# A two-layer diffusion backbone: the output projection and the routing in a fixed order on TensorE, and one product of the first context pair moved to GpSimd

## The chip, the cores and the metric

The kernel runs on one core of a Trainium2 chip. The metric is the device time of one execution in microseconds; the same program is run several times and its median is taken. Engines are called as in the profile: PE (TensorE, matrix products and transpositions), DVE (VectorE), ACT (ScalarE), POOL (GpSimd) and SP (SyncE, which only issues DMAs here). Each executes its own instructions strictly in the order in which they stand, and waits for the others by semaphores.

## The reference

One step of a backbone with 2 layers on 512 latent tokens and 128 context tokens, model width 1024. Every layer mixes tokens and then sends them through 16 experts of which each chooses its own tokens (capacity 64 of 512 latents, 16 of 128 context tokens):

```python
mix = jnp.concatenate([a_out, b_out, c_out], axis=-1) @ w_out
x = layer_norm(ALPHA * x + gate1 * mix, ln1_g, ln1_b)
u = x * (1 + scale2) + shift2
x = layer_norm(ALPHA * x + gate2 * expert_choice_ffn(u, ...), ln2_g, ln2_b)

def expert_choice_ffn(u, w_router, w_gate, w_up, w_down):
    cap = CAPACITY_FACTOR * T // N_EXPERTS
    aff = jax.nn.softmax((u @ w_router).astype(jnp.float32), axis=-1)
    g, idx = lax.top_k(aff.swapaxes(1, 2), cap)
    xs = jax.vmap(lambda ub, ib: ub[ib])(u, idx)
    hdn = jax.nn.silu(xs @ w_gate[e]) * (xs @ w_up[e])     # for each expert e
    ye = hdn @ w_down[e] * g
    # ye is added into the rows idx of a zero tensor of T rows
```

The change touches the stage from the product with `w_out` up to the first expert's products, once in each layer.

## The kernel before, in words

The 640 tokens are five tiles of 128: 0 to 3 are latents, 4 (`CTX`) is the context.

**Projection.** `project(t, half)` makes 512 of the 1024 columns of one tile: 8 steps of k with three 128x512 matmuls each (`mm3`, L229 to L232: high by high, high by low, low by high part), 24 in all, into `ps_o`, of which PSUM holds three. `w_out` is split into high and low parts just ahead of it (L226 on ACT, L227 on DVE or POOL): `wo00`, `wo01` are the two halves of k for the left columns, `wo10`, `wo11` for the right ones. Then DVE multiplies with the gate (L859), adds to the row block `xa` (L861, in layer 1 L864) and takes statistics (L867). After the second half the mean and the inverse deviation `bsd` are made (L300, L284 on DVE, L285 on POOL, L322 on DVE).

**Routing of a tile.** `turn(t, g)` transposes four 128x128 blocks of one half of `xa` on PE (L881), ACT copies them out as `u` (L883), and four 32-row matmuls bring the router's sums into `ps_rt` (L887). `route(t)` copies these (`parts`, ACT, L896), adds them over four groups of partitions by a matmul with `fold` (L898), makes a softmax `rex` on DVE and ACT (L900 to L906; L900 needs `bsd`), transposes it (L907) and copies it to the table of affinities (L909). ACT normalises `xa` in place (L323) and the rows are stored to DRAM as `zrow` (L911), from where the chosen rows are gathered. `residual(t)` later scales `xa` in place (L337, L338 on POOL) and writes it to the accumulator (L842); it overwrites `xa` and so has to wait for the store of `zrow`.

**End of the stage.** When tile 3 is routed, DVE finds the best 64 of the 512 latents for each expert (eight rounds of L976, L979, L980); two small transpositions `ps_tc` on PE turn places (`ldup`) and values (`lvd`) into columns, DVE makes the integer list `lgi` (L1041), and POOL gathers rows (`xsl`, L961). While this goes on, PE does gate and up of the first two experts on their context rows: `fill(n)` issues n of eight groups of four 32-row matmuls into `ps_gc`. `ctx_hidden` makes the hidden rows `hc` from `ps_gc` (silu `sc` on ACT, L1161; product on DVE, L1163), `ctx_turn` transposes them (`ps_hcT`, copied to `hcT` by ACT, L1172), and `ctx_rows` does the down product (`ps_dc`, 16 lines of the program, 32 rows in the trace) and scales it (`yc`, DVE, L1184). Then `xsl` is transposed to `xT` (L253, L261 on ACT, L264 on DVE) and the latent products `ps_g`, `ps_u`, `ps_d` of the pair follow. Seven more pairs of experts follow in each layer.

**What sets the order.** The order on each engine is found by a scheduler that simulates the program; an instruction stands where that simulation lets it start. `inline` (L234 to L239) overrides this for PE: each matmul or transposition given to `mm` or `turn1` is issued after the one given before it. In the kernel before, that holds from the start of the experts' stage on only (`line.clear()` at L1070). The projection and the routing are ordered by the scheduler. The order of DVE, ACT, POOL and SP is the scheduler's throughout, apart from a few `issue_after`.

Of the kernel before, what the change touches and what calls it, by code (L numbers as in the profile page):

```python
# [65 lines left out]
def kernel(ctx: ExitStack, tc: tile.TileContext, a: dict):  # L66
# [162 lines left out]
    def mm3(out, lh, ll, rh, rl, first, last):  # L229
        nc.tensor.matmul(out, lhsT=lh, rhs=rh, start=first, stop=False)  # L230
        nc.tensor.matmul(out, lhsT=lh, rhs=rl, start=False, stop=False)  # L231
        nc.tensor.matmul(out, lhsT=ll, rhs=rh, start=False, stop=last)  # L232
# [543 lines left out]
    def out_proj(l, mixA, mixC, w2, ms, mixed):  # L776
        ps_dn = Banks(f"dn{l}", 2)
# [66 lines left out]
        def project(t, half):  # L844
# [26 lines left out]
        stt, lnv, banks = {}, {}, {}  # L871

        def turn(t, g, after=None, then=None):

            if g == 0:
                banks[t] = ps_dn.tile("ps_rt")
            r = 1 if t == CTX else 0
            ps = ptr("tr8").rearrange("p (k n) -> p k n", k=4)
            with tc.issue_after(after.ins) if after else ExitStack():
                for kk in range(4):  # L880
                    ins = nc.tensor.transpose(ps[:, kk, :], xs[t][0][:, 512 * g + kk:512 * g + 512:4], ident)  # L881
            u2 = newhalf("u2").rearrange("p (k n) -> p k n", k=4)
# [8 lines left out]
        def route(t, after=None):
            r = 1 if t == CTX else 0
            xa, (mv, sd), bank = xs[t][0], lnv[t], banks.pop(t)
            pl, pa = bank[:, 256:256 + NE], bank[0:NE, 384:512]
            parts = newhalf("parts")[:, 0:P]
            nc.scalar.copy(out=parts, in_=bank[:, 0:P])  # L896
            with tc.issue_after(after.ins) if after else ExitStack():
                nc.tensor.matmul(pl, lhsT=parts, rhs=fold, start=True, stop=True)  # L898
            ex = st([P, NE], "rex")
            nc.vector.scalar_tensor_tensor(out=ex, in0=pl, scalar=sd[:, 0:1], in1=lb[:, r], op0=ALU.mult, op1=ALU.add)  # L900
            mx = st([P, 1], "rmx")
            nc.vector.tensor_reduce(out=mx, in_=ex, axis=AX.X, op=ALU.max, negate=True)
            sm = st([P, 1], "rsm")
            nc.scalar.activation(out=ex, in_=ex, func=AF.Exp, bias=mx, scale=1.0, accum_out=sm)
            nc.vector.reciprocal(out=sm, in_=sm)
            nc.vector.tensor_scalar(out=ex, in0=ex, scalar1=sm[:, 0:1], scalar2=None, op0=ALU.mult)  # L906
            order["weighed"] = nc.tensor.transpose(pa, ex, ident)  # L907
            dst = afc if t == CTX else afl[32 * (t // 2):32 * (t // 2) + NE, t % 2 * P:(t % 2 + 1) * P]
            nc.vector.tensor_copy(out=dst, in_=pa)  # L909
            normalise(xa, mv, sd, False)  # L910
# [630 lines left out]
```

## Time and profile before

| | |
|---|---|
| runs of the kernel before | 1294.45, 1296.16, 1302.5 us, median 1296.16 |
| profiled execution | 1294.52 us, span 1292.7 us |
| PE busy | 1193.2 us, 92% of the span |
| DVE, ACT, POOL busy | 543.7, 368.3, 252.8 us (42%, 28%, 20%) |
| chain that ended last | PE 84%, DVE 7%, ACT 4%, DMA 2% |
| stage that is changed | layer 0 from 273.7 to about 372 us; layer 1 the same stage up to 983.6 us |

PE is the engine that the end waits for: any time that it stands idle is in the sum unless something after it waits anyway. The stage is best read in stretches, by how busy each engine is in them, and then by its instructions in order of time.

### The profile page before, as it was taken

To read this page: it belongs to the slowest core of one execution; us is meant where nothing else is said; L and a number is where in the kernel's file an instruction comes from. 1 tells how busy PE (TensorE), PEld (TensorE's weight loads), DVE (VectorE), ACT (ScalarE), POOL (GpSimd) and SP (SyncE) were. 2 spreads that over 40 slices of the span, in tenths; PEclk is the share of its full clock that TensorE was granted. 3 is DMA by queue.
4 is the path that set the end of the run, shared out by engine and by line. 5 is a ranking of instruction groups with operands and counts; after the bars stand their busy time and mean duration, and the time that the engine had idled before them with its cause. 6 is when DMAs were issued, how large, how long until landed. Compare 5 with 4: busy or idle time off the path is not lost.

```text
span 1292.7 us, 18180 instructions
## 1 busy us (share of the span) xinstructions
PE 1193.2 (92%) x7244; PEld 710.7 (55%) x7244; DVE 543.7 (42%) x1266; ACT 368.3 (28%) x800; POOL 252.8 (20%) x234
## 2 busy tenths in 40 slices
PE   5999999999879999999969999999987999999994
PEld 1877886987523333333349998798752333333331
DVE  1554464777531121111297756477653111111116
ACT  1532134663411110111145423475341101011111
POOL 0210002004330221121175000200433022012114
PEclk8999999999979999999989999999998999999998
DMA  9868666164869999999543315606487999999932
GB/s 360 310 209 301 226 237 226 69 214 150 339 259 402 397 396 406 410 400 332 193 138 98 86 46 197 242 19 225 157 320 287 406 396 396 410 406 386 357 102 82
DMA packets 85078, 342.34 MB, mean 265 GB/s; under 512 B 18713, under 2 KB 32089, under 8 KB 54401
## 3 DMA queue, kind: packets, MB, share of 16 engines
q1 hardware_dynamic: 73568, 305.96, 61.4%
q0 software_dynamic: 9840, 29.45, 8.4%
q10 hardware_dynamic: 1584, 5.77, 1.1%
q8 instruction: 57, 0.93, 0.3%
q14 instruction: 29, 0.23, 0.1%
HBM read 313.73 MB, written 27.51 MB: 264 GB/s over the span
## 4 chain that ended last, share of the span: by engine, by line
PE 84%; DVE 7%; ACT 4%; DMA 2%; issue 1%; SPq 1%; POOL 0%; POOLq 0%; ACTq 0%; DVEq 0%
PE ps_d L239 9%; PE ps_g L239 9%; PE ps_u L239 9%; PE ps_gc L239 8%; PE ps_dc L239 5%; PE ps_ada L185 4%; PE ps_c L230 3%; PE ps_c L232 3%; PE ps_c L231 3%; PE ps_o L231 3%; PE ps_o L230 3%; PE ps_o L232 3%; PE ps_p L733 1%; PE tr L239 1%; PE ps_b L230 1%
## 5 line engine op out<-in xcount | busy, mean ns | idle before, releaser
L239 PE MATMUL ps_g<-wg,xT 128*64 128x512 f32 x512 | 116.1, 595 | 0.1
L239 PE MATMUL ps_d<-wd,hT 128*64 128x512 f32 x512 | 113.6, 595 | 2.5 <-DVE yc L1184 1.6
L239 PE MATMUL ps_u<-wu,xT 128*64 128x512 f32 x512 | 115.4, 592 | 0.0
L239 PE MATMUL ps_gc<-wu,xc 128*32 128x512 f32 x512 | 115.0, 595 | 0.0
L239 PE MATMUL ps_gc<-wg,xc 128*32 128x512 f32 x512 | 115.0, 594 | 0.0
L1161 ACT ACTIVATE sc<-ps_gc 32x512 f32<-32x512 f32 x32 | 18.8, 587 | 328.8 <-PE ps_gc L239 299.7
L1163 DVE TENSOR_TENSOR hc<-ps_gc,sc 32x512 f32<-32x512 f32 x32 | 22.0, 688 | 174.9 <-ACT sc L1161 174.8
L239 PEld LDWEIGHTS ps_d<-wd,hT 128*64 128x64 f32 x512 | 35.5, 137 | 78.7 <-issue 75.7
L1110 POOL DMA_INDIRECT yaccc<-yc,csi x28 | 39.8, 1421 | 192.5 <-DVE yc L1184 155.0
L239 PEld LDWEIGHTS ps_g<-wg,xT 128*64 128x64 f32 x512 | 36.0, 137 | 75.1 <-issue 72.7
L239 PEld LDWEIGHTS ps_u<-wu,xT 128*64 128x64 f32 x512 | 37.2, 137 | 72.6 <-issue 71.8
L239 PE MATMUL ps_dc<-wd,hcT 128*32 128x512 f32 x512 | 71.1, 705 | 0.9 <-ACT hcT L1172 0.9
L239 PEld LDWEIGHTS ps_gc<-wg,xc 128*32 128x32 f32 x512 | 29.2, 110 | 75.0 <-issue 73.7
L185 PE MATMUL ps_ada<-wada,cs 128*32 128x512 f32 x368 | 60.1, 630 | 4.8 <-DMA wada<-in_w_ada_dram 4.8
L1212 DVE SCALAR_TENSOR_TENSOR ye<-ps_d,lg,gl 128x512 f32<-128x512 f32 x32 | 24.0, 751 | 95.7 <-PE ps_d L239 92.9
L1191 DVE TENSOR_TENSOR h<-ps_u,sg 128x512 f32<-128x512 f32 x16 | 11.1, 692 | 104.1 <-PE ps_u L239 104.1
L261 ACT ACTIVATE xT<-tr,modB,modA 128x128 f32<-128x128 f32 x64 | 28.0, 459 | 60.8 <-DVE xT L264 59.1
L239 PEld LDWEIGHTS ps_dc<-wd,hcT 128*32 128x32 f32 x512 | 17.2, 126 | 43.0 <-issue 39.1
L961 POOL DMA_INDIRECT xsl<-zrow,lgi x16 | 15.9, 991 | 102.3 <-PE tr L239 87.9
L285 POOL TENSOR_TENSOR bsd<-bsd,neg_half 128x1 f32<-128x1 f32 x15 | 9.5, 634 | 128.7 <-DVE bsd L284 128.7
L1184 DVE SCALAR_TENSOR_TENSOR yc<-ps_dc,cg,gc 128x512 f32<-128x512 f32 x16 | 12.0, 749 | 52.9 <-PE ps_dc L239 52.9
L227 POOL TENSOR_TENSOR wo00l<-r_wo,wo00h 128x1024 fp32r<-128x1024 f32 x4 | 10.4, 2610 | 119.4 <-ACT wo00h L226 119.4
(618 smaller groups left out, 2839.0 us busy)
## 6 DMA issues: line engine op xcount, KB each, us to landing
wg<-in_w_gate_dram SPq DMA_DIRECT2D x64, 1024.0 KB, 12.4
wu<-in_w_up_dram SPq DMA_DIRECT2D x64, 1024.0 KB, 14.9
wd<-in_w_down_dram SPq DMA_DIRECT2D x64, 1024.0 KB, 17.8
wada<-in_w_ada_dram SPq DMA_DIRECT2D x46, 1024.0 KB, 7.2
r_wo<-in_w_out_dram SPq DMA_DIRECT2D x8, 1024.0 KB, 8.7
zrow<-xa ACTq DMA_DIRECT2D x8, 512.0 KB, 7.7
yacc<-xa POOLq DMA_DIRECT2D x8, 512.0 KB, 9.9
z<-yacc SPq DMA_DIRECT2D x8, 512.0 KB, 6.2
```

Of the source, the lines that this page charges most:

```text
L185: nc.tensor.matmul(ps[32 * j:32 * j + 32, :], lhsT=cs[:, k, :], rhs=w[:, j * 512:(j + 1) * 512], start=(k == 0), stop=(k == KD - 1))
L230: nc.tensor.matmul(out, lhsT=lh, rhs=rh, start=first, stop=False)
L231: nc.tensor.matmul(out, lhsT=lh, rhs=rl, start=False, stop=False)
L232: nc.tensor.matmul(out, lhsT=ll, rhs=rh, start=False, stop=last)
L239: line["pe"] = op(*args, **kw)
L261: nc.scalar.activation(out=out[:, kk, :], in_=ps[:, kk, :], func=AF.Identity, scale=A[:, r, k:k + 1], bias=B[:, r, k:k + 1])
L733: nc.tensor.transpose(pt[:, kk, i * P:(i + 1) * P], prs[i][:, (k0 + kk) * P:(k0 + kk + 1) * P], ident)
L961: ins = nc.gpsimd.indirect_dma_start(out=x, out_offset=None, in_=src, in_offset=bass.IndirectOffsetOnAxis(ap=idx, axis=0))
L1110: nc.gpsimd.indirect_dma_start(out=acc[:, :], out_offset=bass.IndirectOffsetOnAxis(ap=idx[h][0:64, j:j + 1], axis=0), in_=y[hs], in_offset ...
L1161: nc.scalar.activation(out=sc[64 * i + 32:64 * i + 64], in_=pc[64 * i:64 * i + 32], func=AF.Silu)
L1163: nc.vector.tensor_tensor(out=hc[32 * i:32 * i + 32], in0=pc[64 * i + 32:64 * i + 64], in1=sc[64 * i + 32:64 * i + 64], op=ALU.mult)
L1212: order["ye"] = nc.vector.scalar_tensor_tensor(out=ye[:, hs], in0=pd, scalar=lg[:, j:j + 1], in1=gl2[:, hs], op0=ALU.mult, op1=ALU.mult)
```

## The change

- `mm3` takes the function that issues its matmuls, and `project` gives it `mm`: all of the projection's matmuls, transpositions and routing matmuls now stand in one written order on PE, from the start of the stage (`line.clear()` is moved there).
- The routing's steps become functions that `project` calls at given steps of k: `turn(t, 0)` at k=4 and `match(t, 0)` (the router's sums) at k=6 of `project(t, 1)`; `turn(t, 1)` and `match(t, 1)` at k=4 and k=6 of the next tile's first half; `weigh` (fold and softmax) at k=0 and `listed` (affinities, normalising, store) at k=5 of its second half. For tile 3 the second half's steps stand between the groups of `fill`.
- The context rows' modulation is divided between DVE and ACT (it was on ACT alone).
- For the first pair, ACT copies the up rows out of PSUM (`uc`), and POOL multiplies them with `sc` into `hc`. The product no longer waits for `lgi`; the scaling `yc` does instead.

```diff
-    def mm3(out, lh, ll, rh, rl, first, last):
-        nc.tensor.matmul(out, lhsT=lh, rhs=rh, start=first, stop=False)
+    def mm3(out, lh, ll, rh, rl, first, last, put=nc.tensor.matmul):
+        put(out, lhsT=lh, rhs=rh, start=first, stop=False)
...
-                mm3(ps, mh[:, k], ml[:, k], wh[:, k % 4], wl[:, k % 4], k == 0, k == KD - 1)
+                for step in between.get(f"k{k}", ()):
+                    step()
+                mm3(ps, mh[:, k], ml[:, k], wh[:, k % 4], wl[:, k % 4], k == 0, k == KD - 1, mm)
...
         project(CTX, 0)
-        project(CTX, 1)
-        turn(CTX, 0)
-        project(0, 0)
-        router(CTX)
...
+        project(CTX, 1, k4=[turn(CTX, 0)], k6=[match(CTX, 0)])
+        for t in range(4):
+            p = t - 1 if t else CTX
+            spare = t in (2, 3)
+            project(t, 0, k1=[ctx_row(t - 2, 0)] if spare else [], k4=[turn(p, 1)], k6=[match(p, 1)])
+            project(t, 1, k0=[weigh(p)], k1=[ctx_row(t - 2, 1)] if spare else [], k4=[turn(t, 0)],
+                    k5=[listed(p)] + ([] if t else [choose]), k6=[match(t, 0)])
+            if t in (1, 2):
+                residual(CTX if t == 1 else 0)
...
-            ins = turn(3, 1, fill(2), lambda ins: fill(1, ins))
-            route(3, fill(1, ins))
-            fill(9, order["weighed"])
+            fill(2)
+            turn(3, 1)()
+            fill(1)
+            match(3, 1)()
+            fill(1)
+            weigh(3)()
+            listed(3)()
+            fill(4)
...
+                    u = pc[64 * i + 32:64 * i + 64]
+                    if pool:
+                        u = uc[64 * i + 32:64 * i + 64]
+                        nc.scalar.copy(out=u, in_=pc[64 * i + 32:64 * i + 64])
+                    (nc.gpsimd if pool else nc.vector).tensor_tensor(out=hc[32 * i:32 * i + 32], in0=u,
...
-                scatter(yaccc, ctx_rows(ctx_turn(ctx_hidden(order["lgi"]))), csi, j)
+                scatter(yaccc, ctx_rows(ctx_turn(ctx_hidden(True)), after=order["lgi"]), csi, j)
```

What this moves on the engines shows at four places of layer 0 (layer 1 has the same). The first is PE at the start of the stage, behind the context tile's left half. Before, one matmul of its right half (`wo10h`) is followed by tile 0's left half:

```order
L232 MATMUL ps_o<-wo01h_2817,ml 128x512
L230 MATMUL ps_o<-wo10h_2835,mh 128x512
L230 MATMUL ps_o<-wo00h_2050,mh 128x512
L231 MATMUL ps_o<-wo00l_2051,mh 128x512
L232 MATMUL ps_o<-wo00h_2050,ml 128x512
```

Now the right half follows at once, with the transpositions of the context tile's `xa` (`tr`) and its router sums within it:

```order
L239 MATMUL ps_o<-wo10l_2836,mh 128x512
L239 MATMUL ps_o<-wo10h_2835,ml 128x512
L239 MATMUL tr_2979<-ident,xa 128x128 x4
L239 MATMUL ps_o<-wo11h_2844,mh 128x512
L239 MATMUL ps_o<-wo11l_2845,mh 128x512
L239 MATMUL ps_o<-wo11h_2844,ml 128x512
```

The right half's low parts and the first half of `xa` are thus needed earlier on PE; the order on DVE, which makes them, is the same as before there (two halves of the split `wo10l`, the left half's gate, two halves of `wo11l`, then `xa`). The second place is PE at the end of the projection. Before, three groups of transpositions and one of router sums stand between the last projection matmul and the second group of `ps_gc`:

```order
L232 MATMUL ps_o<-wo11h_2844,ml 128x512
L881 MATMUL tr_3413<-ident,xa 128x128 x4
L881 MATMUL tr_3461<-ident,xa 128x128 x4
L887 MATMUL ps_rt<-u_3418,wz_2909 32x128 x4
L881 MATMUL tr_3523<-ident,xa 128x128 x4
L239 MATMUL ps_gc<-wg_0_0_3593,xc_2880 32x512
```

After the last projection matmul there now stand two groups of `ps_gc` and then the one transposition that is left:

```order
L239 MATMUL ps_o<-wo11h_2844,ml 128x512
L239 MATMUL ps_gc<-wg_0_0_3593,xc_2880 32x512
L239 MATMUL ps_gc<-wu_0_0_3597,xc_2880 32x512
L239 MATMUL ps_gc<-wg_1_0_3595,xc_2880 32x512
L239 MATMUL ps_gc<-wu_1_0_3599,xc_2880 32x512
L239 MATMUL ps_gc<-wg_0_0_3593,xc_2880 32x512
L239 MATMUL ps_gc<-wu_0_0_3597,xc_2880 32x512
L239 MATMUL ps_gc<-wg_1_0_3595,xc_2880 32x512
L239 MATMUL ps_gc<-wu_1_0_3599,xc_2880 32x512
L239 MATMUL tr_3630<-ident,xa 128x128 x4
```

In all, three of four transpositions, three of four router sums, one of two folds and one of two softmax transpositions have moved ahead of the last projection matmul. The third place is PE behind `fill`, where the order is as it was before (there with the line numbers L989 for L1001):

```order
L239 MATMUL ps_gc<-wu_1_1_3607,xc_2880 32x512
L1001 MATMUL ps_tc<-ident,ldup 128x16
L1001 MATMUL ps_tc<-ident,lvd 128x16
L239 MATMUL ps_hcT<-ident,hc 128x64 x4
L239 MATMUL ps_dc<-wd_0_0_3609,hcT 32x512 x2
```

The transposition of `hc` stands behind both `ps_tc`. The fourth place is POOL's queue. Before, two inverse deviations stand together ahead of a tile's scaling (the last of them is tile 3's):

```order
L285 TENSOR_TENSOR bsd<-bsd,neg_half 128x1
L842 DMA yacc<-xa 128x1024
L285 TENSOR_TENSOR bsd<-bsd,neg_half 128x1
L337 TENSOR_TENSOR xa<-xa,ln_g_2885 128x1024
L338 TENSOR_TENSOR xa<-xa,ln_b_2888 128x1024
L961 DMA xsl<-zrow,lgi 128x1024
```

Now the scaling of tile 2 stands ahead of the `bsd` of tile 3, and the two new products behind it:

```order
L285 TENSOR_TENSOR bsd<-bsd,neg_half 128x1
L337 TENSOR_TENSOR xa<-xa,ln_g_2885 128x1024
L338 TENSOR_TENSOR xa<-xa,ln_b_2888 128x1024
L285 TENSOR_TENSOR bsd<-bsd,neg_half 128x1
L843 DMA yacc<-xa 128x1024
L1178 TENSOR_TENSOR hc<-uc,sc 32x512 x2
L973 DMA xsl<-zrow,lgi 128x1024
```

## Rows read from the trace of the kernel before

**Rows 1.** Busy time by stretch: us, busy per engine, granted clock, DMA share, GB/s.
```profile
273.00:300.00 27.00, 27.00 (x136) 22.29 (x135) 19.68 (x36) 13.40 (x18) 0.56 (x1) 1.00 0.56 201
350.00:361.00 11.00, 3.16 (x32) 0.76 (x24) 10.55 (x45) 0.68 (x2) 4.72 (x2) 0.75 0.35 144
```

**Rows 2.** Waits of PE, 338 to 375 us: total, times, longest.
```profile
PE ps_tc L989 <- DVE ldup L1036: 7.9, 1, 7.9
PE ps_hcT L239 <- DVE hc L1163: 1.8, 1, 1.8
```

**Rows 3.** Timeline, start of the stage: start, duration, engine, line, operation.
```profile
273.67 0.40 PE L230 MATMUL ps_o<-wo00h,mh 128*128 128x512 f32 x1
280.24 1.22 DVE L227 TENSOR_TENSOR wo10l<-r_wo,wo10h 128x1024 fp32r<-128x1024 f32 x1
284.44 0.69 DVE L861 SCALAR_TENSOR_TENSOR xa<-xa,ps_o 128x512 f32<-128x512 f32 x1
```

**Rows 4.** Timeline of PE: routing steps among projection matmuls.
```profile
298.70 0.64 PE L881 MATMUL tr<-ident,xa 128*128 128x128 f32 x4
299.40 0.40 PE L231 MATMUL ps_o<-wo00l,mh 128*128 128x512 f32 x1
...
302.25 0.43 PE L887 MATMUL ps_rt<-u,wz 128*32 128x128 f32 x8
```

**Rows 5.** Timeline from the last projection matmul to the search's first instruction.
```profile
338.68 0.39 PE L231 MATMUL ps_o<-wo11l,mh 128*128 128x512 f32 x1
338.90 0.39 PE L232 MATMUL ps_o<-wo11h,ml 128*128 128x512 f32 x1
...
340.07 0.69 DVE L861 SCALAR_TENSOR_TENSOR xa<-xa,ps_o 128x512 f32<-128x512 f32 x1
...
345.02 1.24 ACT L323 ACTIVATE xa<-xa,bnb,bsd 128x1024 f32<-128x1024 f32 x1
...
346.64 0.24 ACT L896 COPY parts<-ps_rt 128x128 f32<-128x128 f32 x1
...
349.94 0.42 DVE L976 MAX8 tav<-affl 48x8 f32<-48x256 f32 x1
```

**Rows 6.** POOL's scaling of tile 2, timeline.
```profile
351.12 2.38 POOL L337 TENSOR_TENSOR xa<-xa,ln_g 128x1024 f32<-128x1024 f32 x1 [8.56 <-DMA zrow<-xa]
```

**Rows 7.** Stores of zrow: page, DMA issues (last number us to landing).
```profile
zrow<-xa ACTq DMA_DIRECT2D x8, 512.0 KB, 7.7
```

**Rows 8.** The tile zrow, its stores and gathers together.
```profile
DMA to landing us min/median/max: 2.6/9.0/11.4
```

**Rows 9.** Timeline of PE after the search, layer 1.
```profile
976.33 0.71 PE L239 MATMUL ps_hcT<-ident,hc 64*128 64x64 f32 x4 [1.80 <-DVE hc L1163]
```

**Rows 10.** Timeline of ACT in layer 0, ahead of the latent rows' modulation.
```profile
370.79 1.06 ACT L333 ACTIVATE ln_g<-ln_g 128x1024 f32<-128x1024 f32 x1 [5.08 <-DMA ln_g<-in_ln_g_dram]
372.20 1.87 ACT L261 ACTIVATE xT<-tr,modB,modA 128x128 f32<-128x128 f32 x4 [0.35 <-DVE xT L264]
```

**Rows 11.** The costliest groups: down products of the latents, all pairs.
```profile
L239 PE MATMUL ps_d<-wd,hT 128*64 128x512 f32 x512 | 113.6, 595 | 2.5 <-DVE yc L1184 1.6
```

**Rows 12.** DVE and POOL side by side, 311 to 316 us.
```profile
312.03 2.85 DVE L227 TENSOR_TENSOR ml<-mixA,mh 128x512 fp32r<-128x512 f32 x1
...
311.94 2.38 POOL L338 TENSOR_TENSOR xa<-xa,ln_b 128x1024 f32<-128x1024 f32 x1
```

**Rows 13.** DVE in the search, beside the scaling of rows 6.
```profile
351.72 0.40 DVE L979 MATCH_REPLACE8 affl<-tav,taa 48x256 f32<-48x256 f32 x1
```

**Rows 14.** Timeline of PE: the same product in two later pairs.
```profile
456.86 3.64 PE L239 MATMUL ps_dc<-wd,hcT 128*32 128x512 f32 x32
...
491.42 0.82 PE L239 MATMUL ps_hT<-ident,h 128*128 128x128 f32 x4 [1.23 <-ACT xT L261]
492.17 5.20 PE L239 MATMUL ps_dc<-wd,hcT 128*32 128x512 f32 x32
```

**Rows 15.** Busy time in the second of them, columns of rows 1.
```profile
492.00:495.00 3.00, 3.00 (x18) 0.79 (x20) 0.42 (x1) 0.37 (x1) 0.00 (x0) 0.50 1.02 431
```

More of the change, by code (lines that the diff above doesn't have):

```diff
@@ L842, in residual, with project @@
             nc.gpsimd.dma_start(out=acc_rows(t), in_=res)
-        def project(t, half):
+        def project(t, half, **between):
             r = 1 if t == CTX else 0
@@ L891, in route @@
[L891 to L910, printed above, removed]
-            ins = (nc.sync if t == CTX else nc.scalar).dma_start(out=zrowc if t == CTX else zrow[t * P:(t + 1) * P, :], in_=xa)
-            if t == CTX:
-                order["store"] = ins
@@ new lines, in match, with step @@
+        def match(t, g):
+            def step():
+                if g == 0:
+                    banks[t] = ps_dn.tile("ps_rt")
+                r = 1 if t == CTX else 0
+                for kk in range(4):
+                    at = NE * (4 * g + kk)
+                    mm(banks[t][32 * kk:32 * kk + 32, 0:P], lhsT=wz[:, r, at:at + 32], rhs=turned[t][:, kk, :], start=(g == 0), stop=(g == 1))
+                if g == 1:
+                    turned[t] = newhalf("parts")[:, 0:P]
+                    nc.scalar.copy(out=turned[t], in_=banks[t][:, 0:P])
+            return step
@@ new lines, in listed, with step @@
+        def listed(t):
+            def step():
+                xa, pa = xs[t][0], banks.pop(t)[0:NE, 384:512]
+                turn1(pa, chosen.pop(t), ident)
+                dst = afc if t == CTX else afl[32 * (t // 2):32 * (t // 2) + NE, t % 2 * P:(t % 2 + 1) * P]
+                nc.vector.tensor_copy(out=dst, in_=pa)
+                normalise(xa, *lnv[t], False)
+                ins = (nc.sync if t == CTX else nc.scalar).dma_start(out=zrowc if t == CTX else zrow[t * P:(t + 1) * P, :], in_=xa)
+                if t == CTX:
+                    order["store"] = ins
+            return step
@@ new lines, in choose, with ctx_row, step @@
+        def choose():
+            ctxr.extend(route_ctx(rt, rx, afc))
+            xsc.extend(gather(newrow("xsc", "crow"), zrowc[:, :], ctxr[0][:, hf:hf + 1]) for hf in range(2))
+        def ctx_row(hf, g):
+            def step():
+                ps = ptr("tr8").rearrange("p (k n) -> p k n", k=4)
+                for kk in range(4):
+                    turn1(ps[:, kk, :], xsc[hf][:, 512 * g + kk:512 * g + 512:4], ident)
+                modulate(xc[:, 4 * g:4 * g + 4, hf * P:(hf + 1) * P], ps, A, B, 1, g)
+            return step
@@ L1060, in experts @@
         nslot, paced = [0], []
-        line.clear()
         def eload(src, shape, name):
```

83 lines of the change are left out of this document (33 added, 50 removed).

## The prediction

> **What bounds the kernel now.** PE does. I read the stretches first, for where it stands idle; then its waits, for whom; then the timeline of the changed stage. From 273 to 300 us PE is busy for all 27.00 us at full granted clock [rows 1]: where the projection begins, the order in which the work stands on PE costs nothing now. From 350 to 361 us it is busy for 3.16 of 11 us while DVE is busy for 10.55: here DVE's search for the best 64 latents sets the end, and PE waits 7.9 us for its list [rows 1, 2]. Then comes a wait of 1.8 us for `hc`, the product that now goes to POOL [rows 2]. So in this stage the end is set by PE up to the last projection matmul, by a chain through DVE, ACT and POOL up to the search's first instruction, by the search, and by short hand-overs behind it. Each microsecond that the search starts later is paid, whatever PE does meanwhile.
>
> **The change, part by part.** All of it happens twice, once a layer.
>
> *Start of the stage: +3.2.* Matmuls start every 0.23 us (338.68, 338.90 [rows 5]). The stage starts at 273.67, and the context tile's right half starts after 24 of them and a small one, at about 279.3. Its second matmul wants the first half of `wo10l`. DVE takes up the second half at 280.24 [rows 3], so the first is ready just before that: a wait of about 0.8. After 12 matmuls more, at 279.3 + 0.8 + 12 x 0.23 = 282.9, stands the transposition of the context tile's `xa`, and `xa` is ready at 284.44 + 0.69 = 285.1 [rows 3]: a wait of 2.3. Nothing stands by for PE, since the order is fixed; before, tile 0's left half stood there. The order on DVE is unchanged at this place, so neither wait can shrink much; I put the bounds at 2.5 and, if the clock falls after the wait as below, at 4.8.
>
> *Work moved ahead of the last projection matmul: +3.2.* Three groups of transpositions, three of router sums, a fold and a small transposition. A group of transpositions and the matmul behind it take 299.40 - 298.70 = 0.70 us, so the group adds 0.47; the sums take about 0.43 [rows 4]; the two single matmuls a quarter of a group each, 0.2 together (an estimate). 3 x 0.47 + 3 x 0.43 + 0.2 = 2.9, and the matmuls next to each group start some 0.05 later: 3.2. The last projection matmul thus moves by 6.4.
>
> *From there to the search: -2.6.* Before, 349.94 - 338.90 = 11.04 us [rows 5]. Now, counted from the last matmul: `xa` is ready after 340.07 + 0.69 - 338.90 = 1.9. Then two groups of `ps_gc` stand ahead of the transposition (32 matmuls, that is 8 groups, in 3.16 us [rows 1], so 0.8), which adds 0.65 with its pipe; ACT copies `u`, half the elements of a normalisation of 1.24 [rows 5], so 0.6: 3.95. On ACT tile 3's normalisation now stands ahead of `parts`: 5.2. From `parts` to the search it takes 349.94 - 346.64 = 3.3 [rows 5]: 8.5 instead of 11.0. So what was moved ahead costs more in front than the chain behind gives back.
>
> *POOL's queue: +1.0.* Tile 3's `bsd` now waits behind the scaling of tile 2, which waits for the store of `zrow` to land, as the wait of 8.56 us shows [rows 6]. Tile 2's normalised rows are ready about 5 us after its last matmul (1.9, then 1.8 of statistics and `bsd`, then 1.24). The last matmul of tile 3 comes 48 x 0.23 + 3.2 = 14.2 us after the last of tile 2; so the store is issued 9.3 before it. Landing takes 7.7 [rows 7], and two scalings of 2.38 [rows 6] end 3.2 after that last matmul, where `bsd` is wanted at 2.9. A landing of 2.6 costs nothing and one of 11.4 costs 4 [rows 8]. Transfers are dense here, so I take 1.0. Behind tile 1's scaling tile 2's `bsd` waits in the same way, but its softmax is wanted by PE only some 6 us later, which covers it.
>
> *Behind the search: -1.8 in layer 1, -0.3 in layer 0.* `hc` is made on POOL while DVE searches. Its price has no row: between a scaling of the same kind, 2.38 for 1024 columns [rows 6], and, by half the columns, 1.2; I take 1.2, and two are 2.4. ACT is busy for 0.68 of 11 us and POOL for 4.72 [rows 1], and the scaling of tile 2 will be over, so even two of 2.38 are hidden; without that cover they would cost what they last. The wait for `hc` goes [rows 2, 9]. But the order on PE shows that `ps_hcT` and the down product stay behind both `ps_tc`: only these 1.8 us are won. In layer 0 even they are not. There the latents' modulation on ACT stands behind the scaling of `ln_g`, which waits 5.08 us for a load and ends at 370.79 + 1.06 = 371.85, while the modulation starts at 372.20 now [rows 10]: 0.3. This load follows POOL's work behind the gather, which the change leaves where it is.
>
> *Modulation of the context rows on two engines, and the expert pairs' end: -1.6.* The first has slack. In pair 6 of layer 1, DVE now scales the context rows ahead of the latents' and the wait of 1.6 us for `yc` goes [rows 11].
>
> *The sum.* Per layer 3.2 + 3.2 - 2.6 + 1.0 = +4.8; with the gains behind the search +4.5 and +3.0; less 1.6: **+5.9**. The profiled execution took 1294.5, so 1300.4; the median of the runs is 1296.2, 1.7 above it, and gives 1302.1. I forecast **1301.5**.
>
> *A rule that speaks against it.* The search on DVE did not wait for POOL: MATCH_REPLACE8, with two tiles in SBUF to read, took 0.40 us beside a scaling of 2.38 that had begun before it [rows 6, 13]. A subtraction of two SBUF tiles on DVE did wait: 2.85 us beside POOL's scaling, about as long as that one took [rows 12]. The Trainium skill, "SBUF — State Buffer", section "Who interferes with whom", states that a DVE instruction with two SBUF inputs and a GpSimd instruction that reads SBUF exclude each other for the whole instruction. For the subtraction the trace agrees; for the search it doesn't, and the trace decides: I add nothing for `hc`. By the rule the third rival would be the forecast.
>
> **The rivals.**
>
> 1. *The store lands late.* If `zrow` needs 11.4 us [rows 8], `bsd` of tile 3 costs 4 and tile 2's is no longer covered (some 3 more): about +6 a layer over my 1.0, so 1313. For it: the landings' median over stores and gathers is 9.0 [rows 8]. Against: stores alone have 7.7 [rows 7]. It decides from a landing of about 9.
>
> 2. *Faster than before: the later pairs keep their clock.* In the pair at 492 us PE waits 1.23 us, the granted clock then falls to 0.50, that is 1.2 instead of 2.4 GHz, and the down product takes 5.20 us; in another pair it takes 3.64 [rows 14, 15]. Six of the fourteen pairs look like the slow one. The change shifts when each pair starts; if none fell it would give 6 x 1.56 = 9.4: 1292. It decides from about four of the six. Against: the waits themselves stay, and as many pairs may fall that don't now.
>
> 3. *`hc` on POOL holds up the search.* If DVE's search had to wait for POOL as the subtraction did, two products add up to 2 x 1.2 a layer, 4.8 in all: 1306. Rows 13 speak against it.
>
> 4. *The down product goes into the search.* That would be the change doing more than I say: 1.8, the 0.7 of `ps_hcT` and 5 us of `ps_dc` a layer would leave the path, about -12 against my sum: 1289. The order on PE excludes it.
>
> **How the numbers follow.** Forecast 0.62, its own range 1296 to 1307 (start 2.5 to 4.8, landing 2.6 to 9); late store 0.15; clock 0.14; `hc` 0.05; down product 0.02; the rest 0.02. The range of 8 in 10 takes in most of the late store and of the clock: 1291 to 1312. One per cent of 1296.16 is 13 us, which is what a measurement of this kernel can tell from no change: faster means under 1283, slower over 1309. Under 1283 lies only a mixture of the second and the fourth rival: 0.03. Over 1309 lies most of the late store: 0.12. The rest, 0.85.
>
> **What would show it.** In the changed profile PE should wait for `wo10l` and then 2 to 2.5 us for `xa` about 9 us after the stage starts; the last projection matmul should come 71 to 73 us after the first instead of 65; the search's first MAX8 8 to 10 us after that; no wait for `hc`; `ps_hcT` right behind the second `ps_tc`. I am wrong if PE is busy throughout the first 27 us, if the search starts less than 2 us later than before, counted from the stage's start, or if tile 3's `bsd` stands waiting for over 3 us.

## The result, and the profile after

The changed kernel takes 1309.78 us (median of 8 runs, 1306.28 to 1314.11) against 1296.25 for the kernel before (8 runs on the same chip): ratio 1.0100, interval 1.0077 to 1.0124. The direction was as forecast and the time lies inside the range of 8 in 10, but outside my own range of 1296 to 1307: the loss is 13.5 us where I had worked out 5.3 over the median of the runs. The profiled execution took 1309.33, its span is 1307.5. Runs of one kernel differ by up to 11 us here, and a profile is of one of them, so its time is given below where it lies more than 3 us from the median.

First the page of the changed kernel: busy time (share, instructions), the stores of `zrow` (KB each, us to landing) and the group that answers to rows 11; then the line of the tile `zrow` that answers to rows 8.

```profile
PE 1204.3 (92%) x7244; PEld 709.4 (54%) x7244; DVE 546.1 (42%) x1278; ACT 367.6 (28%) x788; POOL 258.4 (20%) x238
zrow<-xa ACTq DMA_DIRECT2D x8, 512.0 KB, 8.3
L239 PE MATMUL ps_d<-wd,hT 128*64 128x512 f32 x512 | 115.1, 603 | 0.9 <-ACT hT L1215 0.9
```

```profile
DMA to landing us min/median/max: 8.3/8.6/9.2
```

The wait of the down products for `yc` [rows 11] is gone, and stores and gathers land in 8.3 to 9.2 us where they took 2.6 to 11.4 [rows 8]. The waits of PE from 270 to 395 us (in all, times, longest) answer to rows 2:

```profile
PE ps_tc L1001 <- DVE ldup L1048: 7.9, 1, 7.9
...
PE tr L239 <- DVE xa L865: 0.7, 1, 0.7
```

The search's wait is what it was. New are the two waits at the stage's start (0.4 for `wo10l`; 2.3 put down to "issue", where the transposition of the context tile stands; DVE has its `xa` done just before, as shown below), and 0.7 for `xa` among the projection matmuls. The wait for `hc` is no longer there. `ps_hcT` waits 0.5 for `lg` instead: in the code it shares one PSUM buffer with `ps_tc`, which DVE must read first.

The stage's times, each a difference of two starts in the timeline, from the first projection matmul `ps_o`: to the last one, from there to the first MAX8 of the search (called the tail below), from MAX8 to the first `ps_tc` behind it, from there to the first `ps_g` of the expert pairs, the sum of these, and from `ps_g` to the start of the last pair's `ps_d` (all in us):

| kernel, layer | last ps_o | to MAX8 | search | to ps_g | first ps_g | pairs |
|---|---|---|---|---|---|---|
| before, 0 | 65.23 | 11.04 | 11.10 | 11.18 | 98.55 | 260.2 |
| after, 0 | 73.83 | 10.55 | 11.11 | 10.13 | 105.61 | 260.6 |
| before, 1 | 65.18 | 11.04 | 11.10 | 10.80 | 98.12 | 262.1 |
| after, 1 | 73.20 | 9.40 | 11.10 | 10.71 | 104.42 | 263.7 |

So layer 0 lost 7.5 us and layer 1 lost 7.9. Outside these stretches the two profiled executions differ by +1.0 ahead of layer 0, -0.9 between the layers and -0.7 at the end: together that is the 14.8 between 1294.52 and 1309.33.

The start of the stage in the timeline of PE, with the wait ahead of an instruction in brackets after it, DVE's `xa` that the second wait is for, and the first landmark of the end:

```profile
280.33 0.39 PE L239 MATMUL ps_o<-wo10h,mh 128*128 128x512 f32 x1
281.14 0.50 PE L239 MATMUL ps_o<-wo10l,mh 128*128 128x512 f32 x1 [0.42 <-DVE wo10l L227]
281.48 0.40 PE L239 MATMUL ps_o<-wo10h,ml 128*128 128x512 f32 x1
...
285.42 0.68 DVE L865 SCALAR_TENSOR_TENSOR xa<-xa,ps_o 128x512 f32<-128x512 f32 x1
286.19 0.72 PE L239 MATMUL tr<-ident,xa 128*128 128x128 f32 x4 [2.27 <-issue]
...
348.47 0.39 PE L239 MATMUL ps_o<-wo11h,ml 128*128 128x512 f32 x1
```

This answers to rows 3 and 5. A wait costs more than it lasts: from 280.33 to 281.48 are 1.15 us, with the wait of 0.42 and two intervals of 0.23 in it, so 0.27 are lost besides. Behind the second wait the clock did not fall in this execution, as busy time by stretch shows (columns of rows 1; the clock is the last but two):

```profile
286.20:289.00 2.80, 2.80 (x20) 2.00 (x21) 0.62 (x1) 0.59 (x1) 0.00 (x0) 1.00 0.93 322
```

The routing steps that now stand among the projection matmuls, in the timeline of PE; they answer to rows 4:

```profile
344.53 0.40 PE L239 MATMUL ps_o<-wo10h,ml 128*128 128x512 f32 x1
344.77 0.64 PE L239 MATMUL tr<-ident,xa 128*128 128x128 f32 x4
345.16 0.48 PE L239 MATMUL ps_o<-wo11h,mh 128*128 128x512 f32 x1
345.48 0.39 PE L239 MATMUL ps_o<-wo11l,mh 128*128 128x512 f32 x1
...
346.52 0.40 PE L239 MATMUL ps_o<-wo11h,ml 128*128 128x512 f32 x1
346.85 0.43 PE L239 MATMUL ps_rt<-u,wz 128*32 128x128 f32 x8
347.20 0.50 PE L239 MATMUL ps_o<-wo11h,mh 128*128 128x512 f32 x1
347.54 0.40 PE L239 MATMUL ps_o<-wo11l,mh 128*128 128x512 f32 x1
```

From 344.53 to 345.48 are 0.95 us with two intervals of 0.23 in it, so a group of transpositions adds 0.49; from 346.52 to 347.54 are 1.02, so a group of sums adds 0.56. The first had been priced at 0.47, the second at 0.43, and all of them together at another 0.3 for the matmuls behind them. Measured in the same way the kernel before has 0.49 and 0.56 too: a step costs no more in the fixed order than among work that PE can choose from. The matmul behind a step lasts 0.48 to 0.50 instead of 0.40.

From the last projection matmul to the search in layer 0, all engines; this answers to rows 5 and 6:

```profile
339.99 0.33 ACTq L922 DMA_DIRECT2D zrow<-xa  x1
...
349.57 2.36 POOL L337 TENSOR_TENSOR xa<-xa,ln_g 128x1024 f32<-128x1024 f32 x1 [11.46 <-DMA zrow<-xa]
...
351.32 0.15 DVE L284 TENSOR_SCALAR bsd<-bmv 128x1 f32<-128x1 f32 x1
352.01 2.37 POOL L338 TENSOR_TENSOR xa<-xa,ln_b 128x1024 f32<-128x1024 f32 x1
...
354.34 0.55 POOL L285 TENSOR_TENSOR bsd<-bsd,neg_half 128x1 f32<-128x1 f32 x1
...
354.92 0.16 DVE L322 SCALAR_TENSOR_TENSOR bnb<-bmv,bsd 128x1 f32<-128x1 f32 x1 [3.45 <-POOL bsd L285]
...
359.02 0.42 DVE L988 MAX8 tav<-affl 48x8 f32<-48x256 f32 x1
```

The store of tile 2 is issued at 339.99 and POOL begins to scale that tile at 349.57. DVE has its half of tile 3's `bsd` done at 351.47; POOL takes it up at 354.34, when both scalings are over: 2.9 us lost. The same place in layer 1 has a `bnb` that waited 2.30 for `bsd` instead of 3.45, and a tail 1.15 shorter.

Behind the search: PE in layer 0, then the same product in layer 1. They answer to rows 9 and 14.

```profile
370.12 0.28 PE L1001 MATMUL ps_tc<-ident,ldup 16*128 16x16 f32 x1 [7.89 <-DVE ldup L1048]
372.39 0.71 PE L239 MATMUL ps_hcT<-ident,hc 64*128 64x64 f32 x4 [0.53 <-DVE lg L1065]
373.57 5.48 PE L239 MATMUL ps_dc<-wd,hcT 128*32 128x512 f32 x32 [0.46 <-ACT hcT L1187]
...
990.18 6.08 PE L239 MATMUL ps_dc<-wd,hcT 128*32 128x512 f32 x32 [0.46 <-ACT hcT L1187]
```

`hc` is made in good time, and the wait of 1.80 [rows 9] has become 0.53. But the down product behind it takes 5.48 and 6.08 us, where the same product takes 3.64 in a pair that keeps its clock [rows 14].

### The profile page after: what moved, and what is told of

The parts are those of the page before. It is cut to its first block, busy times and chain, and to the rows that moved or that the text cites. A ratio compares the mean times of both kernels' runs of the same rounds, so it can differ in the third digit from the quotient of the medians.

```text
span 1307.5 us, 18183 instructions
## 1 busy us (share of the span) xinstructions
PE 1204.3 (92%) x7244; PEld 709.4 (54%) x7244; DVE 546.1 (42%) x1278; ACT 367.6 (28%) x788; POOL 258.4 (20%) x238
## 4 chain that ended last, share of the span: by engine, by line
PE 81%; DVE 8%; DMA 3%; ACT 3%; issue 2%; POOL 1%; SPq 1%; ACTq 0%; POOLq 0%; DVEq 0%
PE ps_d L239 9%; PE ps_g L239 9%; PE ps_u L239 8%; PE ps_gc L239 8%; PE ps_o L239 5%; PE ps_dc L239 5%; PE ps_ada L185 4%; PE ps_c L230 3%; PE ps_c L232 3%; PE ps_c L231 3%; PE tr L239 2%; PE ps_p L733 1%; PE ps_a L232 1%; DMA zrow<-xa 1%; PE ps_a L230 1%
## 5 line engine op out<-in xcount | busy, mean ns | idle before, releaser
L1178 DVE TENSOR_TENSOR hc<-ps_gc,sc 32x512 f32<-32x512 f32 x28 | 19.3, 688 | 173.7 <-ACT sc L1173 173.6
L239 PE MATMUL ps_dc<-wd,hcT 128*32 128x512 f32 x512 | 74.1, 731 | 0.9 <-ACT hcT L1187 0.9
L1121 POOL DMA_INDIRECT yacc<-ye,lgi x14 | 19.8, 1411 | 81.1 <-DVE ye L1228 63.6
L337 POOL TENSOR_TENSOR xa<-xa,ln_g 128x1024 f32<-128x1024 f32 x10 | 23.7, 2373 | 53.4 <-DMA zrow<-xa 38.1
## 6 DMA issues: line engine op xcount, KB each, us to landing
wu<-in_w_up_dram SPq DMA_DIRECT2D x64, 1024.0 KB, 11.4
```

The lines of the kernel that those rows point to most:

```text
L239: line["pe"] = op(*args, **kw)
L337: nc.gpsimd.tensor_tensor(out=out, in0=zh, in1=L["g"], op=ALU.mult)
L1121: nc.gpsimd.indirect_dma_start(out=acc[:, :], out_offset=bass.IndirectOffsetOnAxis(ap=idx[h][0:64, j:j + 1], axis=0), in_=y[hs], in_offset ...
L1178: (nc.gpsimd if pool else nc.vector).tensor_tensor(out=hc[32 * i:32 * i + 32], in0=u, in1=sc[64 * i + 32:64 * i + 64], op=ALU.mult)
```

## The experiments

My theory: the fixed order makes the loss, through work set among PE-bound matmuls, waits there, and POOL's queue; the work on POOL is neutral. Its rival: the products on POOL hold up DVE's search. All kernels ran beside the kernel before, whose medians in these runs were 1296.6 to 1296.9. The diffs are cut to the lines that matter, at the dots. Below, a slow pair is a pair of experts whose down product `ps_dc` takes 5.1 to 5.3 us instead of 3.64, at the lower clock (pair 0 left out, where it is always slower).

**The order alone** (e1_order_only; `hc` stays on DVE).

```diff
...
-                scatter(yaccc, ctx_rows(ctx_turn(ctx_hidden(True)), after=order["lgi"]), csi, j)
+                scatter(yaccc, ctx_rows(ctx_turn(ctx_hidden(order["lgi"]))), csi, j)
```

> The change without its part on POOL: the product hc of the first pair is again made on DVE behind lgi, and yc waits for nothing of its own; the fixed order on PE stays. Theory (the order makes the whole loss: PE waits at the stage's start, steps that cost more when each stands alone among the projection matmuls, and the inverse deviation of tile 3 that waits behind POOL's scaling): about 1311, 1.009 to 1.014 of before, since only about 1.3 us of waiting for hc a layer comes back. Rival (the product on POOL, beside DVE's search or through its copy on ACT, is what costs): 1296 to 1301, 1.000 to 1.004 of before.

It took 1316.53 us (ratio 1.0154, interval 1.0130 to 1.0178), more than I expected: the order makes the loss, and more than all of it. In this kernel's profile the clock fell behind the wait at the start (busy time by stretch, columns of rows 1):

```profile
287.00:290.00 3.00, 2.94 (x14) 2.04 (x18) 0.69 (x1) 0.59 (x1) 0.00 (x0) 0.69 0.93 333
...
289.00:290.00 1.00, 1.00 (x7) 0.35 (x9) 0.00 (x0) 0.00 (x0) 0.00 (x0) 0.50 1.02 434
```

The 0.69 is a mean: from 289 to 290 the clock is 0.50, the lower of the two levels. That was after a wait of 2.25 us; in the changed kernel a wait of 2.27 left it at 1.00. The way behind the search is 1.5 and 1.7 us a layer longer than in the changed kernel, with the 1.81 us for `hc` back. Of the rest, some 5 of the 8.2 us between the two profiled executions, 3.0 stand in layer 1's projection, with two more waits for `xa` (0.78 and 0.40) and a clock of 0.65 and 0.75 from 908.6 to 914.5; why they came I did not settle.

**The work on POOL alone** (e2_pool_only; order as before).

```diff
...
-                scatter(yaccc, ctx_rows(ctx_turn(ctx_hidden(order["lgi"]))), csi, j)
+                scatter(yaccc, ctx_rows(ctx_turn(ctx_hidden(True)), after=order["lgi"]), csi, j)
```

> The kernel before with the part on POOL alone: copy of the up rows on ACT, hc on POOL, yc behind lgi; the order on PE is the scheduler's. Theory: 1292 to 1296, 0.997 to 1.000 of before: the wait for hc shrinks from 1.8 to about 0.5 us a layer, and part of that is lost because the down product then runs longer at the lower clock. Rival (POOL's product costs): 1300 or more.

It took 1296.57 us (1.0001, 0.9986 to 1.0016): no change in the whole, though by its profile the first `ps_g` comes 1.8 and 0.8 us later than before; the stretch between the layers, where nothing was edited, is 4.9 shorter. The search took 13.14 us in both layers instead of 11.10. The timeline shows why; with `hc` ahead of it on POOL, the scaling of a tile slid to this place:

```profile
362.14 2.39 POOL L338 TENSOR_TENSOR xa<-xa,ln_b 128x1024 f32<-128x1024 f32 x1
362.36 2.22 DVE L983 CAST taf<-tai 48x64 f32<-48x64 uint32 x1
```

A cast of 64 columns lasted 2.22 us, to the end of POOL's instruction. So the rival was right that POOL can hold up DVE there, by 2.04 a layer; wrong was which instructions meet: the scaling and a cast, not `hc` and the search's own steps. The Trainium skill, "SBUF — State Buffer", section "Who interferes with whom", lists casts among the DVE instructions that can take the port pair shared with GpSimd, whole instruction against whole instruction. The trace agrees for the cast.

**Tile 3's `bsd` ahead of tile 2's scaling on POOL** (e3_bsd_first).

```diff
...
-                    residual(t, order["last"].ins if t == 3 else None)
+                    residual(t, order["last"].ins if t == 3 else order["bsd3"].ins if t == 2 else None)
```

> The change, with POOL's scaling of tile 2 issued after the inverse deviation bsd of tile 3. Theory: the wait of DVE's bnb for bsd of tile 3 falls from 3.6 and 2.3 us to 0.7, the search starts 2.9 and 1.7 us earlier, and the time falls by 4 to 5 us to about 1305. Rival (the deviation is not on the path: the transposition and sums of tile 3 end as late): the search starts within 0.5 us of where it does in the change, 1309 to 1310.

1307.45 us (1.0081, 1.0062 to 1.0099). The wait on POOL is gone, and a new one stands in its place:

```profile
353.34 0.55 POOL L285 TENSOR_TENSOR bsd<-bsd,neg_half 128x1 f32<-128x1 f32 x1 [13.34 <-DVE bsd L284]
353.86 2.37 POOL L337 TENSOR_TENSOR xa<-xa,ln_g 128x1024 f32<-128x1024 f32 x1
353.92 2.33 DVE L322 SCALAR_TENSOR_TENSOR bnb<-bmv,bsd 128x1 f32<-128x1 f32 x1 [0.66 <-POOL bsd L285]
```

POOL takes up the scaling 0.06 us before DVE's next step, one element a row and 0.16 us long elsewhere, which now ends with it. The tail is 9.99 in layer 0 (10.55 with the wait) and 9.95 in layer 1 (9.40): taking the wait away gained nothing over both, against the 4 to 5 us that I expected. The median is 2.3 us below the changed kernel's, with intervals that overlap. The Trainium skill, "SBUF — State Buffer", section "Who interferes with whom", states that issue order and not the kind of operation decides which of the two is blocked. The trace agrees here: POOL was first, by 0.06 us.

**The context tile's first transposition three matmuls into tile 0** (e4_turn_later).

```diff
-        project(CTX, 1, k4=[turn(CTX, 0)], k6=[match(CTX, 0)])
+        project(CTX, 1)
...
-            project(t, 0, k1=[ctx_row(t - 2, 0)] if spare else [], k4=[turn(p, 1)], k6=[match(p, 1)])
+            project(t, 0, k1=[ctx_row(t - 2, 0)] if spare else [] if t else [turn(CTX, 0)],
+                    k3=[] if t else [match(CTX, 0)], k4=[turn(p, 1)], k6=[match(p, 1)])
```

> The change, with the first transposition and router sums of the context tile moved from k=4 and k=6 of its right half to k=1 and k=3 of tile 0's left half. Theory: the wait of 2.3 us for xa goes and one of about 0.7 us for the split wo11l takes its place, so 1.5 us a layer, about 1307. Rival (the wait for xa only hides the wait for wo11l, which ends as late, so nothing is won): 1309 to 1310.

1303.48 us (1.0043, 1.0023 to 1.0063), less than I expected. The wait of 2.27 is gone; one of 0.22 has come, for the next half of the weights:

```profile
283.54 0.50 PE L239 MATMUL ps_o<-wo11l,mh 128*128 128x512 f32 x1 [0.22 <-DVE wo11l L227]
```

The last projection matmul comes 1.7 and 1.3 us earlier than in the changed kernel, the first `ps_g` 0.9 and 1.1. The medians differ by 6.3 us; of the 4.4 between the profiled executions only these 2.0 stand where the edit is. The pairs lost 1.3, and 2.8 lie between the layers, where nothing was edited.

**The better half by itself: order as before, `hc` on POOL behind the scalings** (f1_hc_last; the scalings of tiles 1 and 2 are also written ahead of it).

```diff
...
-                    (nc.gpsimd if pool else nc.vector).tensor_tensor(out=hc[32 * i:32 * i + 32], in0=u,
-                                                                     in1=sc[64 * i + 32:64 * i + 64], op=ALU.mult)
+                    with tc.issue_after(pool.ins) if pool else ExitStack():
+                        (nc.gpsimd if pool else nc.vector).tensor_tensor(out=hc[32 * i:32 * i + 32], in0=u,
+                                                                         in1=sc[64 * i + 32:64 * i + 64], op=ALU.mult)
...
```

> The kernel before with the part on POOL (as in e2_pool_only), but the two products hc are queued on POOL behind the scaling of tile 2 instead of ahead of it. In e2_pool_only the scaling's second half came so late that it met DVE's cast of the found places (taf): 2.2 us instead of 0.18, and the search took 13.1 instead of 11.1 us. Theory (POOL's instruction and DVE's cast exclude each other): the cast is back at 0.2, the search at 11.1, and the time at about 1292.5, 0.996 to 0.998 of before. Rival (the part on POOL is worth nothing by itself, the slow cast was off the path): 1296 to 1297.

1301.25 us (1.0033, 1.0022 to 1.0044): slower, against what I expected. The mechanism is there, as its timeline shows:

```profile
358.21 2.59 POOL L1168 TENSOR_TENSOR hc<-uc,sc 32x512 f32<-32x512 f32 x2
362.40 0.18 DVE L983 CAST taf<-tai 48x64 f32<-48x64 uint32 x1
```

The cast is back at 0.18, the search at 11.10, and `ps_g` starts 1.1 and 0.7 us earlier than before. The pairs then last 5.9 and 3.2 us longer. In layer 0 most of it is in pair 0, as the timeline of PE shows, and the rest a wait for `yc`:

```profile
391.58 1.13 PE L239 MATMUL ps_hT<-ident,h 128*128 128x128 f32 x4 [2.38 <-ACT xT L261]
```

```profile
PE ps_d L239 <- DVE yc L1190: 3.2, 2, 1.6
```

The activation that PE needs stands behind ACT's scaling of a norm's parameter (`ln_b`), which waits for its load. It did so before too, but the scaling now starts 1.5 us later, counted from the first `ps_g`. The wait for `xT` is 2.38 instead of 1.47, the granted clock is 0.50 from 391.5 to 394 behind it, and pair 0 takes 4.1 us longer. The waits for `yc` [rows 11] are 3.2 instead of 1.6 over both layers; in layer 1 pair 0's `ps_d` takes 8.61 us instead of 7.09, and there are 7 slow pairs instead of 6.

**The same, with `ps_hcT` put ahead of both `ps_tc` on PE and the down product ahead of the second** (f2_turn_early), so that the one runs while DVE searches and the other while the rows are gathered.

```diff
-            latr = route_lat(rt, rx, topk(rx, afl, CAPL, "ta"))
+            best = topk(rx, afl, CAPL, "ta")
+            mid()
+            latr = route_lat(rt, rx, best)
...
```

> f1_hc_last with the transposition ps_hcT ahead of both ps_tc on PE and the down product ps_dc ahead of the second. Theory: the down product begins right behind the list's transposition and runs while the gather of xsl is under way (4.3 us), so that the latents' transposition starts 3 to 4 us earlier in layer 1; in layer 0 the scaling of ln_g on ACT, which waits for its load, still holds the modulation, so there 0.5 us at most: about 1289. Rival (the gather bounds it, or the product at the lower clock takes back what is won): 1292 to 1293.

1295.35 us (0.9982, 0.9967 to 0.9996); the profiled execution took 1291.01. The first `ps_g` comes 2.8 and 2.3 us earlier than before, but the pairs of layer 0 are 5.6 longer. There, as expected, ACT's scaling of `ln_g` still holds the modulation: PE does four matmuls of `ps_g`, waits, and goes on more slowly (12 in 4.49 us, where before 16 took 3.65):

```profile
370.54 1.06 ACT L333 ACTIVATE ln_g<-ln_g 128x1024 f32<-128x1024 f32 x1 [11.05 <-DMA ln_g<-in_ln_g_dram]
...
371.99 4.49 PE L239 MATMUL ps_g<-wg,xT 128*64 128x512 f32 x12 [1.74 <-ACT xT L261]
```

**The same, with the parameters of the next norm behind the second pair's activation on ACT** (g1_ln_late).

```diff
-                L2 = ln_params(ln, l, "ln2_g", "ln2_b", l + 1 < a["depth"])
+                with tc.issue_after(order["sg"].ins):
+                    L2 = ln_params(ln, l, "ln2_g", "ln2_b", l + 1 < a["depth"])
...
```

> f2_turn_early with ACT's scaling of ln_g and ln_b of the second norm moved behind the second pair's silu. Theory: layer 0 now gains what layer 1 gains, 3 us more than f2_turn_early, about 1286. Rival (something else holds the modulation in layer 0, the gather): as f2_turn_early.

**1288.36 us** (0.9951, 0.9929 to 0.9972): faster than both kernels. Its seven runs took 1286.91 to 1294.13, all less than the median of the kernel before. PE behind the search in its timeline:

```profile
358.83 0.74 PE L239 MATMUL ps_hcT<-ident,hc 64*128 64x64 f32 x4 [5.30 <-POOL hc L1171]
361.51 0.25 PE L991 MATMUL ps_tc<-ident,ldup 16*128 16x16 f32 x1 [1.94 <-DVE ldup L1038]
361.69 5.90 PE L239 MATMUL ps_dc<-wd,hcT 128*32 128x512 f32 x30
...
369.91 3.65 PE L239 MATMUL ps_g<-wg,xT 128*64 128x512 f32 x16
```

The down product has gone into the time in which PE waited for the latents' rows, and what is left of it behind `lvd` takes 1.04 us; so it costs little though it is slow. First `ps_g`: 95.88 us in both layers, instead of 98.55 and 98.12. The wait of 1.74 is gone, and the pairs of layer 0 come down from 5.6 over before to 1.9 (a wait for `yc`); those of layer 1 are as before. That makes 3.0 of the 6.2 us between the profiled executions of this kernel and before; 3.5 lie between the layers. There before is the longest of all, 253.1; the others have 247.8 to 252.2. In this kernel a wait for `z` is 1.5 shorter (10.4 to 8.9) and one of 1.1 for a load is missing. That part I can't tie to the edit.

**The order mended** (f3_order_mended): the context tile's transposition later, as above, and besides tile 3's `bnb` made on POOL, its normalisation behind `parts` on ACT, and its right half transposed first.

```diff
...
-                    residual(t, order["last"].ins if t == 3 else None)
+                    residual(t, order["last"].ins if t == 3 else order["bnb3"].ins if t == 2 else None)
...
-            fill(2)
             turn(3, 1)()
-            fill(1)
+            fill(3)
             match(3, 1)()
```

> e4_turn_later with the chain from the last projection matmul to the search mended: the last transposition of tile 3 ahead of the first groups of ps_gc, parts ahead of tile 3's normalisation on ACT, and POOL's scaling of tile 2 behind both the inverse deviation and bnb of tile 3 (bnb is made on POOL for this tile, since in e3_bsd_first DVE's bnb waited 2.3 us beside POOL's scaling). Theory: this chain falls from 10.6 and 9.7 us in e4_turn_later to 7.5, so 5 us in all: about 1298.5, still slower than before by the steps that now lie ahead of the last projection matmul. Rival (another wait takes the place of each one removed): chain over 9 us, 1302 to 1304.

1301.82 us (1.0038, 1.0020 to 1.0056); the profiled execution took only 1296.26. The tail is 9.38 in both layers, against 11.04 before, so the rival of the expectation (over 9 us) held, not the 7.5 of my theory. The router's input is ready well before it is used, and POOL meets DVE once more, now in the softmax:

```profile
348.65 0.59 ACT L891 COPY u<-tr 128x512 f32<-128x512 f32 x1 [5.13 <-PE tr L239]
...
351.14 0.40 PE L239 MATMUL ps_rt<-u,wz 128*32 128x128 f32 x8
352.28 2.34 POOL L340 TENSOR_TENSOR xa<-xa,ln_b 128x1024 f32<-128x1024 f32 x1
...
353.95 0.70 DVE L919 TENSOR_SCALAR rex<-rex,rsm 128x16 f32<-128x16 f32 x1
```

`u` is there at 349.24, the sums start at 351.14, behind the three groups of expert matmuls that I had set ahead of them; `rex` lasts 0.70 instead of 0.23, until POOL is done. First `ps_g` is still 3.8 and 2.8 us later than before.

**The same, with four steps back behind the projection** (h1_steps_back; tile 2's softmax and fold, the transposition and sums of tile 3's left half), tile 2's scaling on POOL behind the gather, and the norm's parameters late as above.

```diff
-            project(t, 1, k0=[weigh(p)], k1=[ctx_row(t - 2, 1)] if spare else [], k4=[turn(t, 0)],
-                    k5=[listed(p)] + ([] if t else [choose]), k6=[match(t, 0)])
+            project(t, 1, k0=[weigh(p)] if t < 3 else [], k1=[ctx_row(t - 2, 1)] if spare else [], k4=[turn(t, 0)] if t < 3 else [],
+                    k5=[listed(p)] * (t < 3) + ([] if t else [choose]), k6=[match(t, 0)] if t < 3 else [])
...
```

> f3_order_mended with four of the routing steps put back behind the last projection matmul, where the kernel before had them: tile 2's fold and softmax transposition, and tile 3's first transposition and router sums (tile 2's scaling on POOL goes behind the gather, and ACT's scaling of ln_g and ln_b behind the second pair's silu). Theory (a step among the projection matmuls is paid in full, behind them it lies in PE's waiting time): the last projection matmul comes 1.5 us earlier after the stage's start than in f3_order_mended (72.0 and 70.5 us there), the chain from it to the search stays at about 9.4, so the search starts 1.5 us earlier (81.4 and 79.8 there), and the time is 1297 to 1300. Rival (the steps are paid wherever they stand): the chain grows by what the projection loses, the search starts within 0.5 us of where it does there.

1303.36 us (1.0053, 1.0033 to 1.0073). The last projection matmul came 1.85 and 0.80 us earlier than in the mended order. Among the matmuls there the four steps add 0.57 + 0.49 + 0.22 + 0.13 = 1.4 us, in full; besides, a wait of 0.27 for `rex` went in layer 0 and one of 0.44 came in layer 1. The tail grew by only 0.13 and 0.12. But this edit also takes POOL's scaling out of the tail, and `rex` lasts 0.23 instead of 0.70 and 0.72. So behind the projection the steps cost about 0.6 of their 1.4 us. The time did not follow: 1303.36 against 1301.82, with intervals that overlap. The profiles say little on this, since that of the mended order is of one of its shortest executions; between them the pairs take 2.9 and 5.0 us longer, with 7 slow pairs instead of 6 and waits of 3.2 for `yc`, as in the better half by itself. (The fastest kernel has those waits too, but 6 slow pairs.)

## Why the prediction came out as it did

Its steps against the two layers, in us (the pairs' line: the wait for `yc` that goes, and the clock):

| step | predicted | layer 0 | layer 1 |
|---|---|---|---|
| start of the stage | +3.2 | +2.7 | +2.6 |
| rest up to the last projection matmul | +3.2 | +5.9 | +5.4 |
| from there to the search, with POOL's queue | -1.6 | -0.5 | -1.6 |
| the search | 0 | 0 | 0 |
| behind the search | -0.3, -1.8 | -1.0 | -0.1 |
| the pairs | 0, -1.6 | +0.5 | +1.6 |
| sum | +4.5, +1.4 | +7.5 | +7.9 |

*Right in mechanism and nearly in size.* PE waited at the two places named, 0.42 and 2.27 us instead of 0.8 and 2.3 (which add up to 3.1, not 3.2). "Nothing stands by for PE" holds, as moving the transposition shows. The search did not grow; the third rival did not come true in this kernel, but only because POOL's scaling fell earlier: the order as before with the work on POOL has a delay of that kind, 2.04 a layer, through the scaling and a cast.

*MATCH_REPLACE8 was misread, and with it what the rule would make of the search.* I took it for an instruction with two tiles to read. Just ahead of it the trace has one that loads the eight values to be replaced:

```profile
351.64 0.08 DVE L979 MATCH_VALUE_LOAD affl<-tav,taa 48x8 f32 x1
```

So MATCH_REPLACE8 itself may read one tile only. Then its running beside the scaling does not speak against that rule, and by the rule, too, the third rival was not the forecast. No run here tests this.

*The step that failed: "Work moved ahead of the last projection matmul: +3.2".* This is the largest miss, 4.9 us over both layers. The steps themselves were priced nearly right: 3 x 0.49 + 3 x 0.56 + 0.3 = 3.5 by the changed kernel's own rows. I had put two things at nothing. A fixed order waits in the middle of the projection too: 1.2 us in layer 0 (0.70 for `xa`, 0.28 for `parts`, 0.24 for `rex`), 0.5 in layer 1 (0.27 for `parts`, 0.25 for `rex`). And behind each wait, those at the start included, 0.16 to 0.27 us more are lost until the matmuls start every 0.23 us again, 1.2 for the five of layer 0 and 1.0 for the four of layer 1. That is all of the 5.9, and 5.0 of the 5.4; the rest I did not find.

*The pairs: 3.7 us over both layers.* The 1.6 for `yc` was won (pairs 6 and 7 of layer 1 are 1.8 nearer together). But there are 7 slow pairs instead of 6, which is 1.7. In layer 1 pair 0's down product lost its clock as well, another 1.7; its line in the changed kernel, that of before, and the stretch within the first:

```profile
1015.29 8.78 PE L239 MATMUL ps_d<-wd,hT 128*64 128x512 f32 x32 [0.46 <-ACT hT L1215]
```

```profile
1001.38 7.09 PE L239 MATMUL ps_d<-wd,hT 128*64 128x512 f32 x32 [0.46 <-ACT hT L1199]
```

```profile
1016.00:1019.00 3.00, 3.00 (x10) 0.89 (x8) 0.00 (x0) 0.00 (x0) 0.00 (x0) 0.50 1.02 429
```

And 0.5 in layer 0 is a wait of 0.22 behind `ln_g`, with what is lost behind it. That is the second rival turned round: I had let pairs only recover, though I wrote that "as many pairs may fall that don't now". Over all kernels here the count of slow pairs is 6 or 7.

*POOL's queue.* Sign and mechanism as forecast, size not: +2.9 in layer 0 and about 1.7 in layer 1 for my 1.0. The store landed in about 9 us instead of 7.7; the stated bounds, 0 to 4, hold it. In layer 0 the 2.9 is just short of the 3 that I had named as a sign of being wrong. Yet without this wait POOL and DVE met two instructions later and gave the gain back, so it was not worth what it lasted.

*Behind the search.* The waits for `hc` went, as I said. In layer 0 the gain was larger than the 0.3 that I allowed: ACT's scaling of `ln_g` waits for its load even longer, to 380.10, and still stands ahead of the modulation, but PE works on the down product until then and waits 0.22 for it. In layer 1 the down product took 6.08 us instead of 4.88 and ate the gain. In layer 0 it starts at the lower clock: in the stretch that ends with its start, busy time by stretch has PE busy for 1.68 of 5.00 us, behind the wait of 7.9, and a granted clock of 0.50, the lower level of 1.2 GHz (in layer 1 it is 0.50 from 982 to 990):

```profile
369.00:374.00 5.00, 1.68 (x10) 1.11 (x14) 2.23 (x14) 0.37 (x1) 2.39 (x2) 0.50 0.14 19
```

*The range* of 8 in 10 held, since I had taken in the late store; the time came out near that rival's price, 1313, but its mechanism came in part only (landings of 8.3 to 9.2 us, not 11.4). That the time lies in the range is luck. Open are: why the clock fell behind a wait of 2.25 us and not behind one of 2.27; which pairs lose it; the stretch between the layers, 247.8 to 253.1 us in the profiles of kernels that have the same work there; and what brought the further waits and the lower clock in layer 1 of the order alone. The reasons for the longer pairs are read from profiles; only the norm's parameters were tried by themselves.

## What to carry to other kernels

Work set by hand among the matmuls of a stage that PE fills is paid in full, with every wait that a fixed order can no longer fill and a little more behind each; behind that stage, where PE waits for a chain of other engines, the same work cost about 0.6 of 1.4 us. So look for the place where PE is idle and move work there: the down product put into the wait for the latents' rows brought the first `ps_g` some 1.6 us forward in each layer, and with the norm's parameters out of its way it made the one version clearly faster than before. And judge an edit by the stages behind it as well: in three of the nine versions the expert pairs, which were not edited, then took over 5 us more than before over both layers.

## What the runs showed of the hardware

- POOL's scaling held up some instructions of DVE until its end, also tiny ones: a cast of 64 columns 2.22 us instead of 0.18, a product of one element a row 2.33 instead of 0.16, a scaling of 16 elements a row 0.70 instead of 0.23. Others it did not: MATCH_REPLACE8 [rows 13], and just ahead of that last scaling, beside the same instruction of POOL, a product that reads PSUM (0.23), a maximum (0.17) and a reciprocal (0.16).
- Behind a wait of 0.24 to 2.27 us among the projection matmuls PE lost another 0.16 to 0.27 us.
- Two products of 32 x 512 on POOL take 2.58 us; I had estimated 2.4.
- Small transpositions and sums among fp32r projection matmuls add 0.49 and 0.56 us a group, before and after, and the next matmul lasts 0.08 to 0.10 longer.
